# Tokens in their natural order inside blocks of 128 rows; S5's order made in the ScalarE copies

## The chip, the core and the metric

The kernel runs on one core of one Trainium2 chip, in one launch. The metric is the time of one execution in microseconds of the device; runs of one kernel on one chip are compared by their median. Everything is float32; products that need it are split in two float32r parts (`hi` and `lo`), so most matrix products are three matmuls.

## The reference, cut to what matters

One layer for a prompt of 2048 tokens (batch 1) and for 8 samples of 8 tokens, width 1024. Only the prompt's tokens are touched by this change.

```python
def hybrid_layer(x, c, r0, s0_re, s0_im, pos0, ...):
    mod = jnp.einsum('bd,de->be', jax.nn.silu(c), w_ada) + b_ada
    sh1, sc1, gt1, sh2, sc2, gt2 = jnp.split(mod[:, None, :], 6, axis=-1)
    h = rms_norm(x, norm1_g) * (1 + sc1) + sh1
    z = jnp.einsum('bld,de->ble', h, w_in)
    q, k, v, g, u, gate_r, gate_s = jnp.split(z, IN_SPLITS, axis=-1)
    q, k = rotary(q, pos), rotary(k, pos) * (RET_DK ** -0.5)
    ret, r_new = retention(q, k, v, r0)                # chunks of 128 tokens, causal mask with decay
    ret = rms_normalize(ret) * jax.nn.silu(g)
    ssm, s_re, s_im = s5(u, s0_re, s0_im, ...)         # a scan over tokens, 32 groups of 16 channels
    ssm = jax.nn.gelu(ssm)
    ssm = ssm * jax.nn.sigmoid(ssm @ w_glu)
    merged = jax.nn.sigmoid(gate_r) * (ret @ w_br) + jax.nn.sigmoid(gate_s) * (ssm @ w_bs)
    x = x + gt1 * (merged @ w_out)
    h2 = rms_norm(x, norm2_g) * (1 + sc2) + sh2
    x = x + gt2 * (jnp.square(jax.nn.relu(h2 @ w_up)) @ w_down)
    return x, r_new, s_re, s_im
y = rms_norm(x, norm_f_g)
```

## The kernel before, in words

**Blocks.** The prompt's 2048 tokens are worked through in four super blocks of 512 tokens (`b` from 0 to 3, `SB` = 512, `P` = 128), each made of four tiles of 128 tokens. After them one feed-forward stage works on all tokens (`feed_forward`, with `w_up` and `w_down` in a seven-product scheme over halves, `ORDER` and `DOWN`, in two passes `k`).

**Order of tokens.** S5 handles eight tokens at once, so it wants u as [channel, s, c], where token = 8c + s. Before the change the kernel makes this order at the door: row r of a 128-token tile holds token 8(r % 16) + r // 16 of that tile. `x_rows` (L1448) loads x in that order, with the pattern [[D, 8], [8 * D, 16], [1, D]] over DRAM, and the stores of y at L529 and L546 write it back with the same pattern. The rotation table, the causal mask and the decays of the retention are computed for that order in `_constants` (`tau`, `tok`).

**Setup** (`setup`, L772). One queue, SP's, issues the DMAs of the whole kernel in program order. In setup it issues constants, two loads `wa` (1 MB each) of the modulation weights, x tile 0, a bias, x tile 1, two more `wa`, x tiles 2 and 3, four more `wa`, and the first weights `wraw`. TensorE (PE) multiplies with `wa` in four groups of 16 matmuls (`ada`, L849), each followed by transposes into `ptm` (L887). ScalarE squares x (`half_square`, L640) as it comes in; VectorE makes the reciprocal root (L644 and after), scales x (L864), PE transposes it (L856), and the first h is made.

**A super block** (`super_block`, L1503) runs the blocks of weights u, q, k, v, g, four gate blocks, glu, br0, br1, bs0, bs1, wo0, wo1. Weights come through `fetch` (L181) as `wraw`, are split by ScalarE (L191) and GpSimd (L194), and are used at L253; results go to four PSUM banks (`pd`) and are evacuated by a function for each block. Small tasks are run between blocks as generators ("fillers"), and the final order of instructions on each engine comes from a simulated timeline.

- u's results are copied from PSUM by ScalarE into `ue` (L1528), in S5's order over the 512 tokens, and stored in DRAM (`usc`). `s5` loads them, scans on VectorE, and stores y to `ysc`.
- Ahead of glu, `yl` is loaded from `ysc`; ScalarE copies it into `gw` (L1630), rounds it into `gh` (L1632), VectorE makes the rest `gl` (L1633), and PE uses `gh` and `gl` in glu.
- Ahead of wo0, four loads of x (`x1`) and, behind them on the queue, the row `gt1` of the modulation (`gt`, 0.5 MB, L926) are issued. VectorE multiplies each bank of wo by `gt` (L1718) and adds x (L1719); then x is stored to `x1d` (L1721). In super block 3 loads of the feed-forward's first parts (`sw`, L390) follow, which ScalarE rounds into `shi` (L396) and VectorE into `slo` (L401).
- `ln1` loads the next super block's x into `xr`, well ahead.

**The end.** In the feed-forward's second pass `output_rows` (L531) takes the rows of the first 1024 tokens from DRAM (`yo`), scales them and stores them (L546, eight stores of 0.5 MB), in a ring of three rows. The other 1024 tokens are finished by `turn_back` (L477): when the last quarter of the columns of four tiles is there, VectorE and ScalarE scale 16 pieces of 128x256 (L526, L528), and SP issues 16 stores of 128 KB (L529), twice.

Of the kernel before, what the change touches and what calls it, by code (L numbers as in the profile page):

```python
# [13 lines left out]
AF = mybir.ActivationFunctionType  # L14
# [3 lines left out]
P = 128  # L18
D = 1024
SB = 512  # L20
# [20 lines left out]
def _constants():  # L41
    f32 = np.float32
    inv = (10000.0 ** (-(np.arange(64) / 64.0))).astype(f32)
    gam = 1.0 - 2.0 ** (-5.0 - np.arange(H))
    sc = 128.0 ** -0.5
    c = np.zeros((P, C_N))
    c[:, C_ID:C_ID + P] = np.eye(P)
    r = np.arange(P)
    tau = 8 * (r % 16) + r // 16
    c[:, C_MASK:C_MASK + P] = tau[None, :] >= tau[:, None]  # L50
    c[:, C_VD:C_VD + H] = gam[None] ** (-(tau[:, None] + 1.0)) * sc
    c[:, C_OD:C_OD + H] = 2.0 * gam[None] ** (tau[:, None] + 1.0)
    c[:, C_OD2:C_OD2 + H] = gam[None] ** (2.0 * (tau[:, None] + 1.0)) / 128.0
    c[:, C_G128:C_G128 + H] = gam[None] ** 128.0
    r = np.arange(64)
    t, b = r // 8, r % 8
    c[:64, C_SMASK:C_SMASK + 64] = (b[None, :] == b[:, None]) & (t[None, :] >= t[:, None])
    ang = ((16384 + t).astype(f32)[:, None] * inv[None]).astype(np.float64)
    c[:64, C_RC:C_RC + 64] = c[:64, C_RC + 64:C_RC + P] = np.cos(ang)
    c[:64, C_RS:C_RS + 64] = -np.sin(ang)  # L60
    c[:64, C_RS + 64:C_RS + P] = np.sin(ang)
    c[:64, C_SVD:C_SVD + H] = gam[None] ** (-(t[:, None] + 1.0)) * sc
    c[:64, C_SOD:C_SOD + H] = 2.0 * gam[None] ** (t[:, None] + 1.0)
    c[:64, C_SOD2:C_SOD2 + H] = gam[None] ** (2.0 * (t[:, None] + 1.0)) / 128.0
    c[:, C_G8:C_G8 + H] = gam[None] ** 8.0
    c[:64, C_BM:C_BM + 8] = b[:, None] == np.arange(8)[None]
    c[112:P, C_L0:C_L0 + 16] = np.eye(16)
    rot = np.zeros((NSB, P, 2, SB))
    pos = np.arange(SB)
    tok = 128 * (pos // 128) + 8 * (pos % 16) + pos % 128 // 16  # L70
    for s in range(NSB):
        ang = ((s * SB + tok).astype(f32)[None, :] * inv[:, None]).astype(np.float64)
        rot[s, :64, 0] = rot[s, 64:, 0] = np.cos(ang)
        rot[s, :64, 1] = np.sin(ang)
        rot[s, 64:, 1] = -np.sin(ang)
    return c.astype(f32), rot.astype(f32)


def raw_ap(t, offset, ap):
    return bass.AP(tensor=t.tensor, offset=t.offset + offset, ap=ap)  # L80


class Layer:
# [393 lines left out]
    def turn_back(self, k, g, i, accs):  # L477

        nc, V = self.nc, self.nc.vector
        acc = accs[g]  # L480
        if i not in self.turned:
            self.turned[i] = [0, self.small(f"ssq{i}", 16)]
            if k and len(self.turned) == 1:
                self.nfg = self.unit("nfg", shape=(P, D))
                nc.sync.dma_start(self.nfg, raw_ap(self.i["norm_f_g"], 0, [[0, P], [1, D]]))
        st = self.turned[i]
        ssq = st[1]
        xs = self.unit("xp", shape=(P, 4, 256))
        t0 = 8 * k + 4 * i
        nc.sync.dma_start(xs, self.x1d[t0:t0 + 4, :, 256 * g:256 * g + 256].rearrange("j p n -> p j n"))  # L490
        rows = acc[:, 2 * i:2 * i + 2].rearrange("p a n -> p (a n)").rearrange("p (t n) -> p t n", n=256)
        pts = []
        for jj in range(2):
            pt = self.bank("pty", [P, 2, 2, P])
            for j in range(2):
                for l in range(2):
                    t = 2 * jj + j
                    nc.tensor.transpose(pt[:, j, l], acc[:, 2 * i + l, P * t:P * t + P], self.ident)  # L498
            pts.append(pt)
        yield 1  # L500
        for n, pt in enumerate(pts):
            V.tensor_add(rows[:, 2 * n:2 * n + 2], pt.rearrange("p j l n -> p j (l n)"), xs[:, 2 * n:2 * n + 2])  # L502
        for t in range(4):
            junk = self.work("junk", [P, 256])
            nc.scalar.activation(junk, rows[:, t], AF.Square, accum_out=ssq[:, 4 * t + g:4 * t + g + 1])  # L505
        if k == 0:
            nc.sync.dma_start(self.yd[4 * i:4 * i + 4, :, 256 * g:256 * g + 256].rearrange("j p n -> p j n"), rows)
        else:
            V.tensor_mul(rows, rows, self.nfg[:, None, 256 * g:256 * g + 256].to_broadcast([P, 4, 256]))
        st[0] += 1  # L510
        if st[0] < 4:
            return
        yield 1
        v = self.small("v4", 4)
        V.tensor_reduce(v, ssq.rearrange("p (t q) -> p t q", q=4), axis=AX.X, op=ALU.add)
        V.tensor_scalar(v, v, 1.0 / D, EPS, op0=ALU.mult, op1=ALU.add)
        r = self.rsqrt(v, 4)
        if k == 0:
            V.tensor_copy(self.rk[:, 4 * i:4 * i + 4], r)
            return  # L520
        yield 1
        for t in range(4):
            for n in range(4):
                o = accs[n][:, 2 * i:2 * i + 2].rearrange("p a n -> p (a n)")[:, 256 * t:256 * t + 256]
                if n < 2:
                    V.tensor_scalar(o, o, r[:, t:t + 1], None, op0=ALU.mult)  # L526
                else:
                    nc.scalar.activation(o, o, AF.Copy, scale=r[:, t:t + 1])  # L528
                nc.sync.dma_start(raw_ap(self.o[0], P * (t0 + t) * D + 256 * n, [[D, 8], [8 * D, 16], [1, 256]]), o)  # L529

    def output_rows(self):  # L531

        nc = self.nc
        u = [self.unit("yo", shape=(P, 2, D)) for _ in range(2)]
        g = u[0][:, 0]
        nc.sync.dma_start(g, raw_ap(self.i["norm_f_g"], 0, [[0, P], [1, D]]))
        row = lambda t: u[(t % 3 + 1) // 2][:, (t % 3 + 1) % 2]
        for t in range(10):
            if t < 8:
                nc.sync.dma_start(row(t), self.yd[t])  # L540
            yield 4
            if t > 1:
                o = row(t - 2)
                nc.scalar.activation(o, o, AF.Copy, scale=self.rk[:, t - 2:t - 1])
                nc.gpsimd.tensor_mul(o, o, g)
                nc.sync.dma_start(raw_ap(self.o[0], P * (t - 2) * D, [[D, 8], [8 * D, 16], [1, D]]), o)  # L546
                yield 2

    def late_norm(self):
# [896 lines left out]


    def x_rows(self, t, b, j):  # L1448
        src = raw_ap(self.i["x_prompt"], (b * SB + P * j) * D, [[D, 8], [8 * D, 16], [1, D]])
        return self.nc.sync.dma_start(t, src)  # L1450

    def xs_rows(self, t):
# [50 lines left out]
    def super_block(self, b, late):  # L1503
        nc = self.nc
        V = nc.vector
        c = self.c
# [18 lines left out]

        def ev_u(j, p):
            t = self.work("ue", [P, 512])
            nc.scalar.activation(t.rearrange("p (s n c) -> p n s c", s=8, n=4),  # L1528
                                 p.rearrange("p (n s c) -> p n s c", s=8, n=4), AF.Copy)
            nc.sync.dma_start(self.usc[j * P:j * P + P], t)  # L1530

        def ev_us(sb):
# [10 lines left out]
        if b == 0:  # L1543
            s5 = self.spawn(self.late_setup, 2)
        self.block("u", "T", srcT(hh, hl), ev_u, S(hS, ev_us))
        if b:
            s5 = self.spawn(self.s5(b), 7)
# [76 lines left out]
        gw = self.unit("gw")  # L1624
        gh, gl = self.unit("gh", F32R), self.unit("gl", F32R)
        ts = []
        for f in range(4):
            t = self.work("yl", [P, 512])
            nc.sync.dma_start(t, self.ysc[f * P:f * P + P])
            nc.scalar.activation(gw[:, f].rearrange("p (n s c) -> p n s c", s=8, n=4),  # L1630
                                 t.rearrange("p (s n c) -> p n s c", s=8, n=4), AF.Copy)
            nc.scalar.activation(gh[:, f], gw[:, f], AF.Copy)  # L1632
            V.tensor_sub(gl[:, f], gw[:, f], gh[:, f])  # L1633
        geS = smS = None
# [78 lines left out]
        def ev_wo(d):  # L1713
            def f(j, p):
                t = self.work("tw", [P, 512])
                e = slice(512 * d, 512 * d + 512)
                x = x1[j // 2][:, j % 2]
                V.scalar_tensor_tensor(t, p, 0.125, gt1[:, e], op0=ALU.mult, op1=ALU.mult)  # L1718
                V.tensor_add(x[:, e], x[:, e], t)  # L1719
                if d:  # L1720
                    nc.sync.dma_start(self.x1d[4 * b + j], x)  # L1721
                    if b < NSB - 1:
                        self.spawn(self.norm_quarters(x, b, j), 20 + 5 * j)
            return f
# [57 lines left out]
        f = self.block("wo1", "N", srcN(mh, ml), ev_wo(1), S(m2S, ev_woS(1)) if smp else None, order=order)  # L1782
# [49 lines left out]
```

## Time and profile before

| what | value |
|---|---|
| median of 3 runs | 3103.24 us (3094.15 to 3113.18) |
| the profiled execution's own time | 3099.62 us |
| its span | 3097.8 us |
| granted TensorE clock, mean | 0.967 |
| DMA | 518.62 MB, mean 167 GB/s |
| loads of x | 20 of 0.5 MB into x0 and x1, 12 into `xr` |
| stores of y | 8 of 512 KB (L546), 32 of 128 KB (L529) |

The span is that of one execution, from the first instruction to the last. PE is TensorE's matmuls, PEld its weight loads, DVE VectorE, ACT ScalarE, POOL GpSimd, SP the queue that issues DMAs; "out<-in" are the names of the tiles, and L12 is a line of the kernel. A row of the timeline has the start, the time taken and, in brackets, how long the engine was idle before and what ended that. A row of a tile or line has the shortest, median and longest duration in ns. A row of waits has the sum, the count and the longest. A row of windows has the busy time of PE, PEld, DVE, ACT and POOL with the number of instructions in brackets, then the granted clock, the busy share of the 16 DMA engines and GB/s.

### The profile page before, as it was taken

The page shows a single profiled execution, that of the slowest core. Times are in us where ns is not written, and L with a number is a line of the kernel's source. Part 1 is how long each engine was busy: PE and PEld are TensorE (multiplying, and loading weights), DVE is VectorE, ACT ScalarE, POOL GpSimd, SP SyncE. Part 2 cuts the span into 40 slices and gives each one's busy share as a digit, 9 for nine tenths or more (in the row PEclk, how much of TensorE's full clock was granted, in tenths as well). Part 3 has the DMA queues.
Part 4 walks back from the last instruction along what each step waited for, and adds up shares of the span by engine and source line. Part 5 has one row for each costly group of instructions (what it writes and reads, how often), then busy time and mean ns, then how long its engine had stood idle before and what let it go on. Part 6 is the DMA issues. An engine that isn't in the chain of part 4 may idle for free. (4 is left out here: it accounts for less than half of the span.)

```text
span 3097.8 us, 37373 instructions
## 1 busy us (share of the span) xinstructions
PE 2911.6 (94%) x13436; PEld 2378.3 (77%) x13436; DVE 1822.8 (59%) x2937; ACT 1407.0 (45%) x2296; POOL 1720.4 (56%) x1036
## 2 busy tenths in 40 slices
PE   7789999999999899999999989999999999998996
PEld 3567787788777778877788778887888788877875
DVE  5978644770575786365842545555556755554655
ACT  2233463322353334534234345566655555566743
POOL 2331464435253644655445477668777666688771
PEclk9889999999999999999999999999999999999998
DMA  8466445643236954447544455556545544466532
GB/s 231 156 192 209 132 128 165 185 110 119 80 92 191 277 181 121 141 137 245 190 133 151 148 191 180 187 197 204 186 154 171 193 168 155 150 220 225 182 128 96
DMA packets 336749, 518.62 MB, mean 167 GB/s; under 512 B 71462, under 2 KB 168246, under 8 KB 332459
## 3 DMA queue, kind: packets, MB, share of 16 engines
q1 hardware_dynamic: 336564, 516.23, 52.6%
q8 instruction: 106, 1.74, 0.2%
q14 instruction: 79, 0.65, 0.1%
HBM read 401.39 MB, written 114.78 MB: 167 GB/s over the span
## 5 line engine op out<-in xcount | busy, mean ns | idle before, releaser
L194 POOL TENSOR_TENSOR wlo<-wraw,whi 128x1024 fp32r<-128x1024 f32 x248 | 616.8, 2498 | 729.0 <-ACT whi L191 585.7
L409 PE MATMUL pq_down<-shi,tw 128*128 128x512 f32 x1792 | 565.5, 395 | 20.7 <-DVE acc L469 10.2
L191 ACT ACTIVATE whi<-wraw 128x1024 fp32r<-128x1024 f32 x312 | 324.4, 1058 | 571.2 <-PE pd_wo L253 63.7
L409 PE MATMUL pq_up<-shi,tw 128*128 128x512 f32 x1792 | 556.9, 391 | 11.9 <-ACT tw L310 8.0
L409 PEld LDWEIGHTS pq_down<-shi,tw 128*128 128x128 f32 x1792 | 340.2, 190 | 96.1 <-ACT acc L467 10.4
L409 PEld LDWEIGHTS pq_up<-shi,tw 128*128 128x128 f32 x1792 | 337.6, 188 | 84.9 <-ACT tw L310 9.2
L311 POOL TENSOR_TENSOR tw<-traw,tw 128x512 fp32r<-128x512 f32 x192 | 274.4, 1442 | 144.7 <-ACT tw L310 144.4
L409 PE MATMUL pq_down<-slo,tw 128*128 128x512 f32 x896 | 353.1, 394 | 0.9 <-DVE slo L382 0.9
L409 PE MATMUL pq_up<-slo,tw 128*128 128x512 f32 x896 | 349.7, 391 | 0.0
L396 ACT ACTIVATE shi<-sw 128x1024 fp32r<-128x1024 f32 x140 | 147.0, 1057 | 167.4 <-DMA sw<-sd 107.9
L469 DVE SCALAR_TENSOR_TENSOR acc<-pq_down,modT,acc 128x512 f32<-128x512 f32 x224 | 161.9, 745 | 95.3 <-PE pq_down L409 95.0
L409 PEld LDWEIGHTS pq_down<-slo,tw 128*128 128x128 f32 x896 | 170.5, 190 | 36.0 <-DVE slo L382 1.4
L409 PEld LDWEIGHTS pq_up<-slo,tw 128*128 128x128 f32 x896 | 168.9, 189 | 34.5
L382 DVE TENSOR_TENSOR slo<-sw,far 128x512 fp32r<-128x512 f32 x160 | 103.7, 682 | 113.3 <-ACT far L381 99.6
L310 ACT ACTIVATE tw<-traw 128x512 fp32r<-128x512 f32 x224 | 137.4, 624 | 54.7 <-PE pq_down L409 39.1
L401 DVE TENSOR_TENSOR slo<-sw,shi 128x1024 fp32r<-128x1024 f32 x60 | 117.7, 1976 | 71.8 <-ACT shi L396 70.6
L419 ACT ACTIVATE aq<-pq_up 128x512 f32<-128x512 f32 x128 | 72.6, 592 | 170.7 <-PE pq_up L409 170.7
L194 DVE TENSOR_TENSOR wlo<-wraw,whi 128x1024 fp32r<-128x1024 f32 x64 | 88.3, 1380 | 73.0 <-ACT whi L191 68.6
L345 POOL TENSOR_TENSOR ts<-traw,ts 128x512 f32<-128x512 f32 x64 | 95.2, 1487 | 53.9 <-issue 49.2
L253 PE MATMUL pd_wo<-whi,mh 128*128 128x512 f32 x256 | 103.9, 410 | 18.9 <-DVE tw L1718 18.9
L310 ACT ACTIVATE tw<-ts 128x512 fp32r<-128x512 f32 x128 | 80.2, 627 | 81.2 <-PE pq_up L409 71.9
L311 POOL TENSOR_TENSOR tw<-t,tw 128x512 fp32r<-128x512 f32 x64 | 88.4, 1387 | 50.2 <-ACT tw L310 50.2
(537 smaller groups left out, 6865.4 us busy)
## 6 DMA issues: line engine op xcount, KB each, us to landing
wraw<-in_w_in_dram SPq DMA_DIRECT2D x144, 512.0 KB
sw<-sd SPq DMA_DIRECT2D x112, 512.0 KB
s5p<-s5c SPq DMA_DIRECT2D x32, 1024.0 KB
traw<-in_w_up_dram SPq DMA_DIRECT2D x64, 512.0 KB
sd<-sq SPq DMA_DIRECT2D x32, 1024.0 KB
sd<-aq SPq DMA_DIRECT2D x32, 768.0 KB
traw<-in_w_down_dram SPq DMA_DIRECT2D x24, 1024.0 KB
wraw<-in_w_ada_dram SPq DMA_DIRECT2D x32, 512.0 KB
```

The source lines that it names most:

```text
L191: a = nc.scalar.activation(hi, raw, AF.Copy)
L194: l = eng.tensor_sub(lo, raw, hi)
L253: nc.tensor.matmul(banks[j], a, b, start=(k == 0 and z == 0), stop=(k == nk - 1 and z == 2))
L310: self.nc.scalar.activation(t[:, 0], x, AF.Copy)
L311: eng.tensor_sub(t[:, 1], x, t[:, 0])
L345: G.tensor_sub(x[p], l, x[m] if isinstance(m, int) else m)
L382: self.nc.vector.tensor_sub(d, a, c)
L396: nc.scalar.activation(hi[:, a], t, AF.Copy)
L401: V.tensor_sub(lo[:, a], t, hi[:, a])
L409: self.nc.tensor.matmul(bank, w, x, start=(first and a == 0 and z == 0), stop=(a == 3 and z == 2), skip_group_check=True)
L419: copy = lambda d, b: nc.scalar.activation(d, b, AF.Copy)
L469: V.scalar_tensor_tensor(d, b, g, d, op0=ALU.mult, op1=ALU.add)
```

## The change

Row r of a tile of 128 now holds token r. Loads of x and stores of y go with one stride over DRAM rows, and the constants are made for that order. The permutation to S5's order moves into the ScalarE copies that already stood there: `ue` now reads PSUM in steps of 8 elements and writes runs, `gw` reads runs and writes SBUF in steps of 8 elements. What is stored in `usc` and `ysc`, and all of S5, stays.

```diff
-    tau = 8 * (r % 16) + r // 16
+    tau = r
...
-    pos = np.arange(SB)
-    tok = 128 * (pos // 128) + 8 * (pos % 16) + pos % 128 // 16
+    tok = np.arange(SB)
...
-                nc.sync.dma_start(raw_ap(self.o[0], P * (t0 + t) * D + 256 * n, [[D, 8], [8 * D, 16], [1, 256]]), o)
+                nc.sync.dma_start(raw_ap(self.o[0], P * (t0 + t) * D + 256 * n, [[D, P], [1, 256]]), o)
...
-                nc.sync.dma_start(raw_ap(self.o[0], P * (t - 2) * D, [[D, 8], [8 * D, 16], [1, D]]), o)
+                nc.sync.dma_start(raw_ap(self.o[0], P * (t - 2) * D, [[D, P], [1, D]]), o)
...
-        src = raw_ap(self.i["x_prompt"], (b * SB + P * j) * D, [[D, 8], [8 * D, 16], [1, D]])
+        src = raw_ap(self.i["x_prompt"], (b * SB + P * j) * D, [[D, P], [1, D]])
...
-            nc.scalar.activation(t.rearrange("p (s n c) -> p n s c", s=8, n=4),
-                                 p.rearrange("p (n s c) -> p n s c", s=8, n=4), AF.Copy)
+            nc.scalar.activation(t.rearrange("p (s c) -> p s c", s=8), p.rearrange("p (c s) -> p s c", s=8), AF.Copy)
...
-            nc.scalar.activation(gw[:, f].rearrange("p (n s c) -> p n s c", s=8, n=4),
-                                 t.rearrange("p (s n c) -> p n s c", s=8, n=4), AF.Copy)
+            nc.scalar.activation(gw[:, f].rearrange("p (c s) -> p s c", s=8), t.rearrange("p (s c) -> p s c", s=8), AF.Copy)
```

## The prediction

> **What bounds the kernel now.** I read the page first, then the windows by 100 us.
>
> ```profile
> span 3097.8 us, 37373 instructions
> PE 2911.6 (94%) x13436; PEld 2378.3 (77%) x13436; DVE 1822.8 (59%) x2937; ACT 1407.0 (45%) x2296; POOL 1720.4 (56%) x1036
> ...
> 0.00:100.00 100.00, 74.16 (x275) 38.30 (x275) 62.63 (x215) 30.78 (x48) 31.47 (x20) 0.94 0.78 221
> 100.00:200.00 100.00, 82.33 (x364) 64.44 (x364) 97.72 (x171) 26.34 (x33) 35.92 (x17) 0.91 0.50 158
> ...
> 2800.00:2900.00 100.00, 92.25 (x392) 73.89 (x391) 54.44 (x84) 68.76 (x105) 76.95 (x58) 0.98 0.63 213
> ```
>
> PE is the bound, but 186 us of the span it is idle (3097.8 - 2911.6), and that idle time sits in places: 26 us in the first 100 us, 8 us around 2850. An edit that touches only transfers can win only there, and at the end. So I asked, for the start, what was waited for, how fast the DMA ran, and in what order PE worked (columns of the timeline: start, duration, what, and in brackets the idle time before it and what ended it).
>
> ```profile
> ACT junk L640 <- DMA x<-in_x_prompt_dram: 21.6, 4, 8.5
> PE ps_ada L849 <- DMA wa<-in_w_ada_dram: 4.9, 1, 4.9
> PE ptm L887 <- DVE v L645: 2.4, 1, 2.4
> ...
> 19.21 0.41 PE L887 MATMUL ptm<-cpk,mt 9*128 9x9 f32 x4 [0.77 <-DVE mt L882]
> ...
> 24.56 9.73 PE L849 MATMUL ps_ada<-wa,z 128*9 128x512 f32 x16 [4.95 <-DMA wa<-in_w_ada_dram]
> 35.73 0.63 ACT L640 ACTIVATE junk<-x 128x512 f32<-128x512 f32 x1 [2.58 <-DMA x<-in_x_prompt_dram]
> 38.42 7.04 PE L849 MATMUL ps_ada<-wa,z 128*9 128x512 f32 x16
> ...
> GB/s 0 0 0 0 0 14 55 55 188 288 228 352 237 133 82 177 266 355 396 382 396 396 416 369 382 403 410 396 410 410 410 369 403 403 239 218 239 218 191 157
> DMA packets 1426, 3.01 MB, mean 251 GB/s; under 512 B 74, under 2 KB 90, under 8 KB 1425
> ```
>
> The GB/s row is the first 12 us in 40 slices. While the weights `wa` come, the queue moves about 400 GB/s; from the slice where the first x rows come it moves about 200. The setup stage waits for x and for `wa` behind x. Next, the price of these issues on the queue of SP, and two windows (last two columns: busy share of the 16 DMA engines, GB/s).
>
> ```profile
> L1450 SPq DMA_DIRECT2D x<-in_x_prompt_dram x20: 588/618/6624, 3.6 to 1732.3; - x20
> L1721 SPq DMA_DIRECT2D x1d<-x x16: 319/338/1927, 506.4 to 1790.5; - x16
> L529 SPq DMA_DIRECT2D out_dram<-acc x32: 598/598/622, 3071.5 to 3093.4; - x32
> L507 SPq DMA_DIRECT2D yd<-acc x8: 359/368/384, 2387.7 to 2438.4; - x8
> ...
> 2755.00:2770.00 15.00, 15.00 (x62) 12.22 (x62) 5.75 (x4) 9.12 (x14) 15.00 (x11) 0.92 1.03 366
> 3080.00:3090.00 10.00, 0.00 (x0) 0.00 (x0) 2.68 (x11) 3.30 (x8) 0.00 (x0) 0.50 0.54 189
> ```
>
> In 3080 to 3090 nothing but stores of y is in flight: half of the engines' time busy, 189 GB/s. In 2755 to 2770 weights and parts are in flight: all busy, 366 GB/s. Bytes per busy engine are the same (189/0.54 = 350, 366/1.03 = 355). So a transfer in the [8][16] order appears to use 8 of 16 engines, and its issue takes 0.60 to 0.62 us where a plain one takes 0.34 to 0.37. [...]
>
> **The change part by part.**
>
> *Loads of x in setup (4).* They go from about 200 to about 400 GB/s. 3.01 MB were moved by 12 us. Up to the end of the third and fourth `wa` load (0.37 + 4 x 1.05 + 2 x 0.52 + 0.07 = 5.7 MB) 2.7 MB remain, 6.9 us at 390 GB/s: 18.9 us, where PE got them at 24.56. The last two x loads are in at 21.6, where ACT got the last at 35.73. PE would begin its second group of 16 at about 19.7 (the transposes `ptm` before it end at 19.62): 4.9 us won. That group took 9.73 us after an idle stretch, its twin at 38.42 took 7.04: 2.7 us more, if the shorter idle time keeps the clock up. The 2.4 us in which `ptm` waits for VectorE, itself held by the last x, go too. Sum 10; low end 5 (the wait alone). What could be late next are the other two weight pairs, 2.1 MB each, in at about 27 and 32 at the same rate; PE comes to them after one and two groups of 7 us and some transposes, at 27.5 at the earliest and after 35: covered.
>
> *Loads of x for x1 (16), at each wo0.*
>
> ```profile
> PE pd_wo L253 <- DVE tw L1718: 18.9, 5, 6.4
> ...
> 470.06 2.77 SPq L1450 DMA_DIRECT2D x<-in_x_prompt_dram  x4
> 472.93 0.40 SPq L926 DMA_DIRECT2D gt<-modd  x1
> ...
> 488.77 1.29 DVE L1718 SCALAR_TENSOR_TENSOR tw<-pd_wo,gt 128x512 f32<-128x512 f32 x2 [10.39 <-DMA gt<-modd]
> 946.44 0.69 DVE L1718 SCALAR_TENSOR_TENSOR tw<-pd_wo,gt 128x512 f32<-128x512 f32 x1 [16.64 <-DMA gt<-modd]
> 1362.25 1.29 DVE L1718 SCALAR_TENSOR_TENSOR tw<-pd_wo,gt 128x512 f32<-128x512 f32 x2 [12.59 <-DMA gt<-modd]
> 1750.79 1.06 ACT L396 ACTIVATE shi<-sw 128x1024 fp32r<-128x1024 f32 x1 [11.49 <-DMA sw<-s2d]
> 1759.79 0.80 PE L253 MATMUL pd_wo<-whi,mh 128*128 128x512 f32 x1 [6.45 <-DVE tw L1718]
> ...
> 940.00:950.00 10.00, 4.99 (x17) 3.72 (x16) 3.45 (x6) 2.23 (x3) 6.98 (x3) 0.74 0.76 216
> 1760.00:1770.00 10.00, 10.00 (x36) 8.10 (x37) 7.79 (x10) 3.55 (x4) 1.36 (x1) 0.80 0.56 168
> ```
>
> `gt` is issued right behind four x loads, on one queue. VectorE's evacuation L1718 waits 10.4, 16.6 and 12.6 us for it in super blocks 0, 1, 2, PE's banks fill up, and PE stops: 18.9 us in all, of which 6.4 in block 3. Four x loads and `gt` are 2.62 MB: 6.7 us at 390 GB/s and, by estimate, 2 us of latency, so `gt` is in at about 479 to 482 instead of 488.77, and so in the others: earlier by more than PE's stop. I take all of 12.5 us (18.9 - 6.4). In block 3 VectorE is held, in its own order, by L401 behind ACT's `shi`, whose loads of s2d stand behind x and `gt`: they come 5.2 us earlier (2.1 MB at 200 and at 400 GB/s), so 5.2 of 6.4. After a stop PE runs at a lower granted clock (0.74, 0.80): 5 x 0.26 + 10 x 0.20 = 3.3 us in these two windows, and I count 5 with their neighbours, an estimate. 12.5 + 5.2 + 5 = 22.7; some will be given back to later waits of VectorE and of the weights' splitting: I take 19. Ends: 8 and 23.
>
> *Loads of x for the next block (12).* PE shows no wait for them; they are issued far ahead. Nothing.
>
> *Stores of y from rows kept in DRAM (8, L546).*
>
> ```profile
> 2774.61 7.88 DMA out_dram<-yo
> ...
> 2783.68 10.13 DMA sw<-sd
> ```
>
> These are two steps of the chain that ended last: a load of the next row waits until a store has landed, and the loads of `sw` stand behind it on SP's queue. Each store is 0.5 MB: 2.6 us at 200, 1.3 at 400 GB/s; eight give back 10 us of the queue. PE is idle 8 us around there (the window above). I take 3, between 0 and 8.
>
> *Last stores (32, L529).*
>
> ```profile
> 3071.49 22.51 SPq L529 DMA_DIRECT2D out_dram<-acc  x32
> ...
> 3080.60 3.30 ACT L528 ACTIVATE acc<-acc,y 128x256 f32<-128x256 f32 x8 [3.55 <-DVE y L634]
> ```
>
> One issue per 0.70 us (22.51/32), 0.60 of it the instruction. The second 16 have their first data at about 3081. With 0.37 + 0.10 each, the first 16 are out by 3079, and the last of the second 16 starts at 3081 + 15 x 0.475 = 3088.1 instead of 3093.4: 5.3 us, and about 0.7 us from a shorter issue and a transfer on twice the engines. I take 6; ends 4.5 and 7. Nothing covers this: after the last store the kernel ends.
>
> *ScalarE copies (32).* They keep their count; the element order changes from runs of 16 to steps of 8 elements, reading PSUM in `ue`, writing SBUF in `gw`. No ScalarE row has such a step. The nearest rows are a pair of VectorE copies of 128x256 from PSUM, one written in steps of 8 elements, one plain.
>
> ```profile
> L1528 ACT ACTIVATE ue<-pd_u x16: 577/602/639, 79.9 to 1414.0; 128x512 f32<-128x512 f32 x16
> L1630 ACT ACTIVATE gw<-yl x16: 612/619/623, 400.6 to 1675.2; 128x512 f32<-128x512 f32 x16
> L1431 DVE COPY rsq<-pis x1: 630/630/630, 780.0 to 780.0; 128x256 f32<-128x256 f32 x1
> L1201 DVE COPY s5hs<-ph x1: 424/424/424, 561.4 to 561.4; 128x256 f32<-128x256 f32 x1
> ...
> 1673.63 2.18 ACT L1630 ACTIVATE gw<-yl 128x512 f32<-128x512 f32 x4
> 1677.02 0.62 PE L253 MATMUL pd_glu<-gh,whi 128*128 128x512 f32 x2
> ```
>
> 0.206 us more for 256 elements is 0.41 for 512: a copy of about 1.02 us. For `ue` that is hidden: a bank of the u block ends every six matmuls, at the 0.23 us from one start to the next about 1.4 us. For `gw` it is not: four copies, then `gh`, `gl` and the evacuations of the last gate that free PE's banks, stand in a row on ScalarE, and PE starts the glu block 1.2 us after the four end (1673.63 + 2.18 = 1675.81). 4 x 0.41 = 1.6 us later, in four super blocks 6.5; some of it has slack. I take 5 lost; ends 0 (no dearer) and 10 (0.62 more per copy).
> [...]
>
> Constants (rotation, mask, decays) change in value only. The order of instructions comes from a simulated timeline, so it may shift somewhere: an estimate of 8 us either way, from PE's waits of 5 to 8 us above.
>
> Sum: -10 - 19 - 3 - 6 + 5 = -33. From the profiled execution's own 3099.62 us (span 3097.8) that is 3066.6; I say 3066. The median of the runs shown is 3103.24, 3.6 us more; 1% of it is 31 us, about what a measurement of this kernel can tell from no change, so "faster by over 1%" means below 3072.
>
> **The rivals.**
> 1. *The stops move.* x comes sooner, but PE, ahead by some us, meets the next late thing: VectorE is busy 97.7 of the 100 us from 100 to 200 (the window above) with S5's setup. Then only the ends and a third of the rest hold: 6 + (10 + 19 + 3)/3 = 17, less 5 for the copies: 3088. For it: VectorE there; against: its work starts earlier too.
> 2. *Slower: the strided copies become the bound ahead of glu.* Place: the four `gw`. At 1.86 us more per copy (four times the time) a block loses 7.4 us, four lose 30, and 16 `ue` of 2.4 us, 1.0 past the 1.4 that a bank takes, another 16; 38 are won without them: 3108. It decides from about 1.6 us more per copy. [...]
> 3. *The halved rate does not come from the order of dimensions.* Then only the issue gets shorter: 4 at the end, 5 lost: 3100. Against: issue time and rate go together in every row.
> 4. *More than counted*, when every stop goes with its clock loss and the copies cost nothing: 10 + 23 + 8 + 7 = 48: 3052, and with an order that turns out well, 3044.
>
> **How the numbers follow.** Forecast 0.52 (3055 to 3080), rival 1 0.25, rival 2 0.08, rival 3 0.06, rival 4 0.09. The range leaves out rivals 2 and 3 and the far end of rival 4: 3044 to 3097 (rival 1 with 8 us of order). Below 3072 lie rival 4 and, of the forecast, nine tenths: 0.56. Slower by over 1% needs more than 3134, copies dearer still than in rival 2, or that with an order that turns out badly: half of rival 2, 0.04. The rest, 0.40, is within 1%.
>
> **What will show it.** Right: an x load and a y store issue at 0.32 to 0.41 us; the last stores run at one per 0.48 us; 400 GB/s while x comes; PE's second group in setup starts near 20 and takes 7 us; no wait of L1718 for `gt` over 5 us; copies near 1.0 us. Wrong: x loads still at 200 GB/s; `gt` in early but PE's wait turned to another name in the same windows; a `gw` copy over 1.5 us and PE waiting for `gh`; or a new order of instructions that moves S5's chain.

## The result, and the profile after

The changed kernel takes 3053.36 us (median of 4 runs, 3046.86 to 3059.84), the kernel before beside it on the same chip 3101.14 us (median of 4, 3094.15 to 3113.18). The ratio is 0.983, with a 95% interval of 0.981 to 0.986: 1.7% faster. The two medians by themselves lie 47.8 us apart, 0.985, inside that interval. The forecast was 3066 us, with a range of 3044 to 3097. The two profiled executions are 3099.62 and 3046.86 us; their spans, 3097.8 and 3045.0, differ by 52.8 us where the sum had 33; the changed kernel's is the fastest of its four, 6.5 us under their median.

The page of the changed kernel, its first two lines and its windows by 100 us for the same stages as before:

```profile
span 3045.0 us, 37372 instructions
PE 2901.0 (95%) x13436; PEld 2374.9 (78%) x13436; DVE 1805.9 (59%) x2937; ACT 1413.8 (46%) x2296; POOL 1729.9 (57%) x1036
```

PE is busy 10.6 us less, though it does the same 13436 matmuls (the clock, below), and idle 144 us in place of 186. To see where the rest went I compared the start of the same group of matmuls in both traces, stage by stage. The distance between the two kernels grows for good in four places; between them it moves by some 4 us either way, which cancels (after setup, for one, it falls from 10.6 to 6.2 us by 411 us):

| stage | forecast | the two profiles | one edit undone alone (below) |
|---|---|---|---|
| setup, to the first matmul of the u block (57.9 to 47.3) | -10 | -10.6 | 14.6 lost, 11.0 of it still there at the end |
| wo0, four super blocks (5.2, 5.5, 7.0, 6.6) | -19 | -24.3 | 24.4 lost |
| second half of the down projection, with the 8 stores of `yo` | -3 | -11.1 | 8.1 lost |
| behind the last down matmul, 32 stores (27.3 to 20.8) | -6 | -6.5 | 6.5 lost |
| copies `ue`, `gw` | +5 | not to be told apart | `gw`: 2 won |

The first four add up to 52.5 of the 52.8 us; what is left over, the copies among it, is near zero in the sum.

PE's own order of instructions changed too. At 826 of the 13436 places of PE's sequence stands a matmul into another tile than in the kernel before, all between 224 and 1129 us of the changed kernel. All runs below in which the loads of x in setup have two strides that don't make one (e4, e5, e9, e10, e11) have the old order, the others the new one.

**Setup.** The window from 11 to 19 us (its last two columns are the share of the 16 DMA engines and GB/s), of the kernel before:

```profile
11.00:19.00 8.00, 7.44 (x15) 1.28 (x13) 0.52 (x1) 1.33 (x4) 0.00 (x0) 1.00 1.05 201
```

The same window of the changed kernel:

```profile
11.00:19.00 8.00, 7.37 (x15) 1.28 (x13) 0.59 (x1) 2.67 (x8) 0.00 (x0) 1.00 1.04 353
```

Its waits in the first 50 us, the one for x:

```profile
ACT junk L639 <- DMA x<-in_x_prompt_dram: 8.9, 3, 5.4
```

And PE's work there, in the timeline, down to the first matmul of u:

```profile
19.14 0.41 PE L886 MATMUL ptm<-cpk,mt 9*128 9x9 f32 x4 [0.77 <-DVE mt L881]
19.48 7.04 PE L848 MATMUL ps_ada<-wa,z 128*9 128x512 f32 x16
...
27.81 7.03 PE L848 MATMUL ps_ada<-wa,z 128*9 128x512 f32 x16
...
47.31 0.50 PE L252 MATMUL pd_u<-hh,whi 128*128 128x512 f32 x1
```

That last row in the kernel before:

```profile
57.92 0.50 PE L253 MATMUL pd_u<-hh,whi 128*128 128x512 f32 x1
```

The wait for `wa` is gone, PE's second group starts at 19.48 and takes 7.04 us, ScalarE waits 8.9 us for x and not 21.6. In both windows the share of the 16 engines is full (1.05 and 1.04), at 201 and at 353 GB/s.

**wo0.** Four windows over wo0 of super blocks 0 to 3 in the kernel before (the third column from the end is PE's granted clock):

```profile
466.00:526.00 60.00, 57.30 (x239) 46.64 (x238) 34.24 (x38) 16.96 (x26) 31.94 (x15) 0.94 0.55 169
909.00:979.00 70.00, 60.02 (x252) 48.76 (x252) 34.76 (x36) 17.07 (x25) 26.26 (x13) 0.93 0.46 133
1337.00:1397.00 60.00, 55.30 (x237) 44.94 (x236) 34.10 (x34) 19.07 (x30) 33.04 (x15) 0.97 0.53 170
1731.00:1801.00 70.00, 55.51 (x222) 44.44 (x221) 39.10 (x38) 26.14 (x32) 28.75 (x17) 0.88 0.70 217
```

The same in the changed kernel, each block's window moved with its start:

```profile
459.00:519.00 60.00, 59.28 (x264) 48.33 (x265) 32.96 (x39) 18.44 (x30) 37.80 (x16) 1.00 0.54 184
895.00:965.00 70.00, 64.68 (x276) 52.89 (x276) 40.94 (x43) 19.07 (x29) 30.04 (x13) 0.95 0.47 149
1314.00:1374.00 60.00, 60.00 (x270) 49.77 (x269) 33.83 (x36) 21.58 (x32) 37.53 (x16) 1.00 0.56 194
1704.00:1774.00 70.00, 60.50 (x252) 48.77 (x252) 41.34 (x39) 27.60 (x34) 35.74 (x22) 0.93 0.67 227
```

And its row among PE's waits, 18.9 us before:

```profile
PE pd_wo L252 <- DVE tw L1715: 2.2, 2, 1.9
```

In the same 260 us PE's idle time falls from 31.9 to 15.5 us (260 less the sum of the busy times). The clock also rises: one minus the clock, times the length of the window, is 18.7 us before and 8.4 after. So 16.3 us come from the waits and 10.3 from the clock, 26.6 in all by the windows, 24.3 by the distance of the groups; by the latter 8 are left for the clock.

**The stores.** A window of 60 us in the kernel before, from four microseconds ahead of the first store of `yo`:

```profile
2770.00:2830.00 60.00, 56.22 (x237) 45.11 (x236) 25.67 (x32) 37.86 (x56) 51.91 (x32) 0.97 0.72 244
```

In its timeline of SP, the load that needs the first store's buffer (that store was issued at 2774.61):

```profile
2782.50 0.32 SPq L540 DMA_DIRECT2D yo<-yd  x1
```

The same window of the changed kernel, four microseconds ahead of its first store too:

```profile
2735.00:2795.00 60.00, 60.00 (x266) 49.57 (x265) 29.97 (x38) 43.49 (x64) 59.37 (x38) 1.00 0.82 278
```

Its timeline of SP, the first store and the load of that buffer, and the 32 last stores in two halves:

```profile
2739.47 0.34 SPq L545 DMA_DIRECT2D out_dram<-yo  x1
2743.05 0.32 SPq L539 DMA_DIRECT2D yo<-yd  x1
...
3025.17 7.73 SPq L528 DMA_DIRECT2D out_dram<-acc  x16
...
3034.65 7.93 SPq L528 DMA_DIRECT2D out_dram<-acc  x16
```

The issues by line (min/median/max in ns):

```profile
L528 SPq DMA_DIRECT2D out_dram<-acc x32: 332/398/407, 3025.2 to 3042.2; - x32
...
L545 SPq DMA_DIRECT2D out_dram<-yo x8: 338/338/338, 2739.5 to 2782.2; - x8
...
L1449 SPq DMA_DIRECT2D x<-in_x_prompt_dram x20: 422/452/3987, 3.6 to 1701.3; - x20
...
L1449 SPq DMA_DIRECT2D xr<-in_x_prompt_dram x12: 340/346/2442, 30.5 to 1284.8; - x12
```

PE does 266 matmuls in 60 us and not 237; at 0.23 us from one start to the next the 29 more are 6.7 us. The step "DMA out_dram<-yo" (7.88 us) is no longer in the chain that ended last. From the issue of the first store to the load of the row that needs its buffer are 3.6 us (2739.47 to 2743.05), where it had been 7.9 (2774.61 to 2782.50).

**The copies.** Their rows by line in the changed kernel (min/median/max in ns):

```profile
L1527 ACT ACTIVATE ue<-pd_u x16: 580/604/643, 69.7 to 1384.5; 128x512 f32<-128x512 f32 x16
L1628 ACT ACTIVATE gw<-yl x16: 1116/1206/1215, 393.8 to 1647.8; 128x512 f32<-128x512 f32 x16
```

And its row among PE's waits that names them:

```profile
PE pd_glu L252 <- ACT gh L1629: 1.4, 3, 1.0
```

`ue`, which reads PSUM in steps of 8 elements, costs what it did (604 ns, 602 before). `gw`, which writes SBUF in such steps, costs twice as much (1206 ns, 619 before), and PE waits 1.4 us for it in the whole kernel.

### The profile page after: what moved, and what is told of

It is laid out like the page before. It is cut to its first block, busy times and chain, and to the rows that moved or that the text cites. A ratio compares the mean times of both kernels' runs of the same rounds, so it can differ in the third digit from the quotient of the medians.

```text
span 3045.0 us, 37372 instructions
## 1 busy us (share of the span) xinstructions
PE 2901.0 (95%) x13436; PEld 2374.9 (78%) x13436; DVE 1805.9 (59%) x2937; ACT 1413.8 (46%) x2296; POOL 1729.9 (57%) x1036
## 4 chain that ended last, share of the span: by engine, by line
PE 75%; DVE 13%; DMA 4%; POOL 3%; issue 2%; ACT 2%; SPq 0%; ACTq 0%; DVEq 0%; POOLq 0%
PE pq_up L408 18%; PE pq_down L408 16%; PE pd_gr L252 6%; PE pd_gs L252 5%; PE pd_wo L252 4%; PE pd_br L252 3%; PE pd_u L252 2%; PE pd_g L252 2%; PE pd_bs L252 2%; PE pd_k L252 2%; PE pd_q L252 2%; PE pd_v L252 2%; PE pd_glu L252 2%; POOL tw L310 1%; DVE s5t L1226 1%
## 5 line engine op out<-in xcount | busy, mean ns | idle before, releaser
L193 POOL TENSOR_TENSOR wlo<-wraw,whi 128x1024 fp32r<-128x1024 f32 x248 | 623.2, 2525 | 714.2 <-ACT whi L190 600.5
L408 PE MATMUL pq_up<-shi,tw 128*128 128x512 f32 x1792 | 557.6, 391 | 10.6 <-ACT tw L309 7.5
L400 DVE TENSOR_TENSOR slo<-sw,shi 128x1024 fp32r<-128x1024 f32 x60 | 110.8, 1863 | 63.7 <-ACT shi L395 60.3
L344 POOL TENSOR_TENSOR ts<-traw 128x512 f32<-128x512 f32 x64 | 87.3, 1365 | 45.6 <-DMA traw<-in_w_up_dram 27.3
```

Of the source, the lines that this page charges most:

```text
L193: l = eng.tensor_sub(lo, raw, hi)
L344: G.tensor_sub(x[p], l, x[m] if isinstance(m, int) else m)
L400: V.tensor_sub(lo[:, a], t, hi[:, a])
L408: self.nc.tensor.matmul(bank, w, x, start=(first and a == 0 and z == 0), stop=(a == 3 and z == 2), skip_group_check=True)
```

## The experiments

My theory: a load or store written as 8 groups of 16 rows moves at little over half the rate (201 GB/s beside 353 in setup's window) and holds what is queued behind it on SP; all of the gain is that, in four places. The rivals: that the order of instructions moved; that the far-apart rows and not the count of groups make a transfer slow; that `gt` and not x1 is what wo0 waits for. Times are medians; ratios are to the kernel before on the same chip.

| run | us | ratio, 95% interval |
|---|---|---|
| e1_yo_stores | 3056.91 | 0.9863 (0.9838 to 0.9888) |
| e2_last_stores | 3055.51 | 0.9850 (0.9831 to 0.9869) |
| e3_x1_loads | 3073.28 | 0.9915 (0.9888 to 0.9942) |
| e4_setup_loads | 3058.15 | 0.9863 (0.9845 to 0.9882) |
| e5_first16 | 3062.61 | 0.9864 (0.9834 to 0.9893) |
| e6_first8 | 3047.73 | 0.9817 (0.9791 to 0.9844) |
| e7_old_gw | 3046.64 | 0.9809 (0.9784 to 0.9834) |
| e9_gt_first | 3084.55 | 0.9940 (0.9918 to 0.9962) |
| e10_near8 | 3088.11 | 0.9944 (0.9928 to 0.9961) |
| e11_near16 | 3054.98 | 0.9837 (0.9814 to 0.9859) |
| e8_gw_read | 3048.72 | 0.9822 (0.9801 to 0.9843) |
| after_again | 3050.83 | 0.9827 (0.9807 to 0.9847) |

How much the same program moves comes first, since everything else is read against it.

> The changed kernel once more, on the chip of the runs beside it: its profile shows by how much the same program's stages move from one execution to the next. Every stage within 4 us of the first profile, and the median within 0.3% of 3053 if the before kernel's is.

Its median is 3050.83; in its profile the stages lie up to 4.8 us from the first one until 2700 us, and 8.1 at the last down matmul, more than I had expected. So a distance at one place of a profile is worth nothing below some 5 us, at the end below some 8; the growth of the distance inside one stage is better (against the first profile the `yo` stage lost 3.7 here, -0.8 to 1.8 in the eight other runs with new stores there).

**One edit undone at a time.**

```diff
-nc.sync.dma_start(raw_ap(self.o[0], P * (t - 2) * D, [[D, P], [1, D]]), o)
+nc.sync.dma_start(raw_ap(self.o[0], P * (t - 2) * D, [[D, 8], [8 * D, 16], [1, D]]), o)   # e1
-nc.sync.dma_start(raw_ap(self.o[0], P * (t0 + t) * D + 256 * n, [[D, P], [1, 256]]), o)
+nc.sync.dma_start(raw_ap(self.o[0], P * (t0 + t) * D + 256 * n, [[D, 8], [8 * D, 16], [1, 256]]), o)   # e2
-            self.x_rows(x1[j // 2][:, j % 2], b, j)
+            self.x_rows(x1[j // 2][:, j % 2], b, j, True)   # e3; e4: the same at the four calls of setup
```

> The changed kernel, with only the 8 stores of `yo` (line L545) in the [8][16] order again; half of y's rows come out permuted. Before and after differ by 11 us in that stage (the distance grew from 35 to 46 us between 2740 and 3010), where the prediction had 3. Theory: these 8 stores alone make the 11 us, because each holds the loads behind it on SP's queue. Then this kernel takes 9 to 11 us more than the changed kernel, all of it between 2740 and 3010, and PE's idle time there comes back. Rival: most of the 11 us is a shift in the order of instructions that reached this stage ahead of its time; then it takes 3 us more or less.

The stage lost 8.1 us, a little under the expected 9 to 11 and nearly three times the rival's 3. The same window in e1:

```profile
2730.00:2790.00 60.00, 56.51 (x239) 45.38 (x238) 25.11 (x32) 38.43 (x57) 52.74 (x34) 0.97 0.73 246
```

And its timeline of SP, the first store and the load that waits for it:

```profile
2734.68 0.66 SPq L545 DMA_DIRECT2D out_dram<-yo  x1
...
2742.57 0.32 SPq L539 DMA_DIRECT2D yo<-yd  x1
```

239 matmuls where the kernel before had 237 and the changed one 266, 246 GB/s as before (244), and 7.9 us again from store to load. These 8 stores alone bring back 8.1 of the stage's 11.1 us. The other 3 stay won in e1 and are not explained; over the whole stage the ten executions with the new stores gain 7.5 to 12.0 us on the kernel before, e1 3.1.

> The changed kernel, with only the 32 last stores (line L528) in the [8][16] order again; the rows of that half of y come out permuted. The two traces differ by 6.5 us in the tail. Theory: each issue takes 0.60 us again and the queue of SP paces the tail at 0.70 us per store; 6 to 7 us more than the changed kernel, all behind the last matmul. Rival: the tail is paced by the arithmetic ahead of the stores, and the gain there came with the earlier stages; then 0 to 2 us more.

From the last down matmul to the end it takes 27.3 us, as before; the changed kernel takes 20.8. The theory's 6 to 7 us, all in the tail. Its timeline of SP:

```profile
3023.76 22.61 SPq L528 DMA_DIRECT2D out_dram<-acc  x32
```

One store every 0.71 us again (22.61/32). In the changed kernel it is one every 0.48 and 0.50 us inside the two halves (7.73/16 and 7.93/16), with 1.75 us between them in which the queue issues nothing.

> The changed kernel, with only the 16 loads of x for x1 at wo0 in the [8][16] order again; x is then added in permuted rows. Theory: the stops of PE in wo0 come from gt queued behind four slow loads; this brings them back, 24 us more than the changed kernel (5 to 7 in each of four super blocks), with PE's wait on L1715 back near 19 us. By the prediction's size it is 19. Rival: the wo0 stages got faster for another reason (the blocks' earlier start, the order of instructions); then under 8 us.

wo0 lost 5.2, 3.5, 8.2 and 7.5 us, 24.4 in all, and PE's wait is back under its name (row among PE's waits in e3):

```profile
PE pd_wo L252 <- DVE tw L1716: 18.7, 5, 6.8
```

The wait grew by 16.5 us (2.2 to 18.7) and the time by 24.4.

> The changed kernel, with only the setup's 4 loads of x in the [8][16] order again; the first 512 tokens are then permuted. Theory: the first matmul of the u block starts 10 us later again (near 58 in place of 47 us), and as 4 us of that were given back in the changed kernel by 355 us, the end comes 6 to 7 us later. Rival: the 10 us come from the second 8 loads or from the order; then the first u matmul stays near 47.

The first matmul of u in e4:

```profile
61.90 0.50 PE L252 MATMUL pd_u<-hh,whi 128*128 128x512 f32 x1
```

61.9 in place of 47.3: 14.6 us, more than expected, and ahead of the first place where PE's order differs. 2.9 of them are made up again at 350 us, ahead of the gate's second half: the stretch between the groups `gs` and `gr` there is 8.3 us in this run and in the kernel before, 11.2 in the changed one. PE waits there for the retention's `rw`, in the kernel before:

```profile
PE prt L1351 <- DVE rw L1347: 2.1, 1, 2.1
```

And in the changed kernel:

```profile
PE prt L1350 <- DVE rw L1346: 4.0, 1, 4.0
```

That wait goes with the order of instructions and not with the time of arrival: it is 2.1 us in all six profiles with the old order, also in e5 and e11, which come to it within 3.1 us of the changed kernel, and 4.0 in all eight with the new one. 11.0 us are left at the end, by one execution of each; e4 undoes the loads and the new order together.

The four ratios lie 0.0031, 0.0018, 0.0083 and 0.0031 above the changed kernel's 0.9832: 0.0163 together, 51 us, of the 52 that its ratio stands for. That ratio's interval (0.0026 either way) enters four times, so this sum is good to some 30 us only. The stages say it more closely: 11.0, 8.1, 24.4 and 6.5 are 50.0 of the 52.8 us.

**gt ahead of x1, in the kernel before.**

```diff
         gt = self.mod_row(gt1)            # moved up
         for j in range(4):
             self.x_rows(x1[j // 2][:, j % 2], b, j)
-        gt = self.mod_row(gt1)
```

> The kernel before, with the load of `gt` issued ahead of the four loads of x1 instead of behind them; nothing else. Theory: PE's stops in wo0 of super blocks 0, 1 and 2 come from gt behind 2 MB at the halved rate; then they go (12 us of PE's 18.9 us of wait on L1718) while those of super block 3, where s2d is behind x too, stay: 10 to 18 us less than the kernel before, though x stays slow. Rival: the evacuation's next step, which adds x1, waits for x itself, so PE stops as long under another name: within 4 us of the kernel before.

PE's wait for L1718 falls from 18.9 to 8.0 us, all of that in super block 3, and VectorE no longer waits for `gt`. The row among PE's waits in e9:

```profile
PE pd_wo L253 <- DVE tw L1718: 8.0, 1, 8.0
```

And its timeline of VectorE, the first L1718 of super block 0:

```profile
491.86 1.29 DVE L1718 SCALAR_TENSOR_TENSOR tw<-pd_wo,gt 128x512 f32<-128x512 f32 x2 [4.39 <-PE pd_wo L253]
```

Super blocks 0, 1 and 2 win 4.7, 5.6 and 5.9 us, block 3 hardly any (0.5 until its first feed-forward matmul). By the ratio it is 0.6% faster, some 19 us. So `gt`, behind slow loads, was the cause in three blocks. x1 itself does come late in two of them (VectorE waits for it at L1719, 8.7 us in seven stretches of blocks 1 and 2), and PE does not stop for it. In block 3 it is what else stands behind x: VectorE's L401 still waits for ScalarE's `shi`, and that for the loads of `s2d`. VectorE's row in e9's timeline:

```profile
1745.72 2.47 DVE L401 TENSOR_TENSOR slo<-sw,shi 128x1024 fp32r<-128x1024 f32 x2 [9.57 <-ACT shi L396]
```

And ScalarE's:

```profile
1744.63 1.06 ACT L396 ACTIVATE shi<-sw 128x1024 fp32r<-128x1024 f32 x1 [9.10 <-DMA sw<-s2d]
```

**What makes a transfer slow.**

```diff
-        src = raw_ap(..., [[D, P], [1, D]])
+        src = raw_ap(..., [[D, 16], [16 * D, 8], [1, D]])    # e5 (and both stores)
+        src = raw_ap(..., [[16 * D, 8], [D, 16], [1, D]])    # e6 (and both stores)
+        src = raw_ap(..., [[15 * D, 8], [D, 16], [1, D]])    # e10
+        src = raw_ap(..., [[7 * D, 16], [D, 8], [1, D]])     # e11
```

> The changed kernel, with all loads of x and stores of y written as two strides again, but with 16 groups of 8 rows ([D,16],[16D,8]) where the kernel before has 8 groups of 16; the tokens are then permuted inside 128 rows, which changes the numbers and not the amount of work. Theory: what counts is how many groups the first dimension has, so 16 groups move at the full rate (about 400 GB/s at the start, first u matmul near 47 us), and only the dearer issue of a two-stride transfer stays: 32 last stores at 0.70 us instead of 0.48, so 5 to 7 us more than the changed kernel, near 3059. Rival: what counts is that rows which follow each other in memory go to places far apart; then it is as slow as the kernel before in every stage, 40 to 50 us more.

> The changed kernel, with all loads of x and stores of y in natural order, but written as 8 groups of 16 rows ([16D,8],[D,16]): the same bytes to the same places as in the changed kernel. Theory: if the first dimension as written decides, they go at 200 GB/s again and take 0.60 us to issue, and the time is that of the kernel before less the difference of the copies, 45 us more than the changed kernel. Rival: the two strides are one (16 times D is the next group), the transfer is seen as 128 rows, and the time is that of the changed kernel within 3 us; then this says nothing of the count of groups and only the run with 16 groups does.

> The changed kernel, with all 32 loads of x as 8 groups of 16 rows that follow each other in memory ([15D,8],[D,16]: groups overlap by a row, so that the two strides don't become one; some rows of x are read twice and some not, the amount of work is the same). Stores as in the changed kernel. The run with 16 groups of far rows came out between before and after: first u matmul at 50.1 (47.3 and 57.9), 250 GB/s while x came. Two things differ there: how many groups, and how far apart the rows of a group are. Theory: the count decides, 8 groups are slow wherever their rows are: first u matmul at 57 or later, 200 GB/s between 11 and 19 us, PE's stops in wo0 back, 30 us more than the changed kernel. Rival: the distance decides; then within 5 us of the changed kernel, but for dearer issues.

> The changed kernel, with all loads of x as 16 groups of 8 rows that follow each other in memory ([7D,16],[D,8], overlapping by a row; some rows of x are read twice and some not). Theory that the count decides alone: as the run with 16 groups of far rows, first u matmul at 50. Rival, that both count and distance matter: near 47.5, as the changed kernel, though its issues take 0.55 us; then the 3 us in between are the far rows' own.

The window from 11 to 19 us, and under it the issues of x by line, in e5:

```profile
11.00:19.00 8.00, 8.00 (x14) 1.41 (x13) 0.00 (x0) 2.67 (x8) 0.00 (x0) 1.00 1.04 270
...
L1449 SPq DMA_DIRECT2D x<-in_x_prompt_dram x20: 542/596/3894, 3.6 to 1712.0; - x20
```

The same in e10, with its row among PE's waits:

```profile
11.00:19.00 8.00, 8.00 (x15) 1.37 (x13) 0.00 (x0) 1.33 (x4) 0.00 (x0) 1.00 1.05 171
...
L1449 SPq DMA_DIRECT2D x<-in_x_prompt_dram x20: 588/615/7931, 3.6 to 1741.2; - x20
...
PE pd_wo L252 <- DVE tw L1715: 21.4, 4, 7.6
```

The same in e11:

```profile
11.00:19.00 8.00, 7.44 (x16) 1.28 (x13) 0.52 (x1) 2.67 (x8) 0.00 (x0) 1.00 1.03 267
...
L1449 SPq DMA_DIRECT2D x<-in_x_prompt_dram x20: 541/594/3256, 3.6 to 1712.6; - x20
```

e6 says nothing of the count: its issues of x take 366 ns at the least, 435 in the median (452 in the changed kernel, 596 in e5), and its time is the changed kernel's, as if its two strides were one. The others do. With 8 groups it is slow even where each group's rows lie side by side: 171 GB/s, first u matmul at 65.3, 21.4 us of stops in wo0, 37 us slower than the changed kernel beside it (3050.83). With 16 groups the first u matmul is at 50.1 (far rows) and 49.9 (near rows), and the stops in wo0 stay away (2.8 us of wait on L1715 in e5, 4.2 in e11). So the count of groups decides here (8: 201 and 171 GB/s, 16: 270 and 267), and the distance of the rows makes no difference that shows. (e10 and e11 have the same order of instructions, so that is not between them.) What neither theory had: 16 groups reach 270 and 267 GB/s in this window, not the 353 of one stride. In e5, whose stores have 16 groups too, the `yo` stage loses 5.2 us and the tail 3.8, and it comes out 0.47 points above e6, some 15 us, where I expected 5 to 7 (the two differ in the order of instructions as well). That loss of the two-stride form at 16 groups is measured and not explained.

**The price of gw.**

```diff
-nc.scalar.activation(gw[:, f].rearrange("p (c s) -> p s c", s=8), t.rearrange("p (s c) -> p s c", s=8), AF.Copy)
+nc.scalar.activation(gw[:, f].rearrange("p (n s c) -> p n s c", s=8, n=4),
+                     t.rearrange("p (s n c) -> p n s c", s=8, n=4), AF.Copy)   # e7
+nc.scalar.activation(gw[:, f].rearrange("p (c s) -> p c s", s=8), t.rearrange("p (s c) -> p c s", s=8), AF.Copy)   # e8
```

> The changed kernel, with the copy to `gw` in runs of 16 elements as in the kernel before, so that the order of S5's output is not undone there; nothing else. It prices the strided write: 16 copies of 1.21 us each become 0.62 us. Theory: 0.6 us per copy is exposed only partly; 2 to 4 us less than the changed kernel (PE's wait for gh there is 1.4 us in all). By the prediction's way of counting, four copies in a row per block, it would be 16 times 0.59, 9 us less. Rival: it is hidden, 0 to 1.

Its copy takes 618 ns again. Across the four glu blocks the distance to the changed kernel moves by -0.7, 1.1, -0.7 and -1.6 us: about 2 won. Its ratio is 0.0008 under that of e6 beside it, 2.5 us, well inside the intervals. The theory's 2 to 4 fits, 9 does not.

> The changed kernel, with the copy to gw turned round: it reads the SBUF tile in steps (of 64 elements) and writes gw plainly, the same values in the same places. Theory: on ScalarE steps on the side that is read cost nothing, as in ue (0.60 us, PSUM), and steps on the side that is written do (1.21 us): gw takes 0.62 us again and the kernel is 0 to 3 us faster than the changed kernel. Rival: it is steps in SBUF that cost, read or written: 1.2 us again and no difference.

The rival holds (the copy's row by line in e8):

```profile
L1628 ACT ACTIVATE gw<-yl x16: 1074/1122/1132, 391.7 to 1645.6; 128x512 f32<-128x512 f32 x16
```

Reading SBUF in steps of 64 elements costs nearly what writing it in steps of 8 does (1122 and 1206 ns), and the time is that of the changed kernel. No version tried beats it by more than the scatter.

## Why the prediction was right, and where its steps failed

- **Setup, -10: right, 10.6.** The second group at 19.48 (said: near 20), 7.04 us long (said: 7); while x came, the window shows 353 GB/s (said: 400, the rate of the `wa` loads in the kernel before). That the size fits is partly luck: the profile that the sum was made from has the earliest first u matmul of the four with 8 groups (57.9; the others 61.9, 65.3 and 67.0), and e4 puts the same loads at 14.6. Not counted: 2.9 us given back at 350 us, which go with the new order of instructions.
- **wo0, -19: the cause right, the size off; 24.3.** The stops that were to go did go (18.9 to 2.2 us). The mis-sized term is the clock, "I count 5 with their neighbours": 8 to 10 us. The deduction from 22.7 to 19 for what would be given back did not happen. The 2 us of latency are what `cc` takes at the start of the kernel before (32 KB, issued at 1.15 us; ScalarE waits for it until 3.15); for `gt` itself no run shows them, but VectorE's waits for it fall from 39.6 to 7.3 us. In e3 as in the pair, each us of PE's wait came with half a us more of time.
- **Stores of `yo`, -3: the step that failed; 11.1, and 8.1 by e1.** It priced the queue (2.6 us and 1.3 us per store at the two rates) and then took a part of PE's idle time. But the row loop holds its buffer until the store has landed, and that was 7.9 us and is 3.6. The row with 7.88 us was quoted in the prediction, as a step of the chain that ended last; its saving should have been taken from there, several times over (argued from the rows; e1 shows only what the eight stores cost together).
- **Last stores, -6: right, 6.5.** A store goes out every 0.48 and 0.50 us inside the halves (said: 0.475), the second half starts 9.5 us behind the first (3025.17 to 3034.65; said: 3071.5 to 3081), and from the first issue to the last are 17.0 us where there were 21.9: 4.9 won on the queue (said: 5.3). The issue takes 0.40 us, not 0.37; the other 1.6 us lie behind the last issue. There 0.7 had been set down, in part for "a transfer on twice the engines", a number that no run shows; what shows is a share of 0.54 at 189 GB/s among the last stores before (3080 to 3090), and of 0.67 at 221 in the changed kernel (3030 to 3040).
- **Copies, +5: the direction right, the size too large.** 1.02 us was said for both. `ue` takes 0.60, `gw` 1.21, and of the 9 us that the 16 `gw` add, some 2 reach PE (e7). VectorE's pair, 630 and 424 ns, read PSUM plainly and wrote SBUF in steps: its extra, 0.206 us for 256 elements, was also that of a written side.
- **"Uses 8 of 16 engines", worked out from 189 GB/s at a share of 0.54:** it fits the stores alone at the end. In setup the share of the engines was 1.05 at 201 GB/s, full at little over half the rate of the changed kernel. The count of groups is shown to decide (171 GB/s with 8 in e10, 267 with 16 in e11); how many engines a transfer used no run shows. Why the share is full all the same, and whether the weights queued beside x slow down with it, is open. The issue of an x load takes 0.45 us in setup's and wo0's queue, 0.35 for `xr`; 0.32 to 0.41 had been said.
- **Rivals.** 1 (stops move): not seen; the 2.9 us at 350 us are the order's. 2 (copies bind): it needed 1.6 us more per copy; 0.6 came. No run shows its four times the time: `gw` took twice (1206 ns, 619 before). 3 (not the order of dimensions): refuted by e10 and e11. 4 (more than counted), at 3052 with a chance of 0.09, is where the run fell, one us from its time by the median (its terms add to 48, the two profiles differ by 52.8): every stop did go with its clock loss. Its copies were not quite free, and the stores of `yo` gave more than its 8. The shift of the order of instructions that I allowed 8 us for did come, and its one visible price is the 2.9 us. From 160 us to wo0 of super block 2, less the two wo0 in between, the eight executions with the new order gain -3.3 to 6.3 us on the kernel before, the five others with the old one -1.6 to 4.7, so what it is worth in all does not show above the scatter.

The sum falls 20 us short of the two profiles (33 against 52.8): 8 in the stores of `yo`, 5 in wo0, 1 in setup and tail together, and 5 that were set down for the copies, of which some 3 were never lost and the rest came back between the stages.

## What to carry to other kernels

When a profile shows a share of DMA that is full while the rate is low (here 1.05 at 201 GB/s, beside 1.04 at 353 with one stride), look at how the slow transfer's outer dimension is written, then at what small load stands behind it on the queue: here 128-row loads written as 8 groups cost 24 us at wo0 through the loads behind them, and moving one of these, a row of factors, ahead of x won two thirds of it without touching x. Price a faster store by what waits for its landing (here the time from store to load fell from 7.9 to 3.6 us), not by its share of the queue. And where a stop of PE is removed, add to it for the clock, if the windows around such stops show it reduced; here it was half of the stop again (8.0 us beside 16.3). Last, compare the order of instructions too when a scheduler makes it: here an edit of transfers changed 826 places of PE's sequence.

## What the runs showed of the hardware

- A ScalarE copy of 128x512 that reads PSUM in steps of 8 elements costs nothing more (604 ns against 602); one that writes SBUF in steps of 8, or reads it in steps of 64, costs nearly double (1206 and 1122 against 619).
- The slow loads are also uneven: the first u matmul came at 57.9, 61.9, 65.3 and 67.0 us in four executions whose setup loads had 8 groups (the kernel before, e4, e10, e9), and between 47.3 and 48.5 in all eight with one stride.
- In wo0 the clock gave back half to two thirds as much as the stops themselves (8.0 us by the distance of the groups, 10.3 by the windows, beside 16.3).
